# A decoder layer's distance bias, made on 128 partitions with 32x32 products and two VectorE additions, after norm1's output instead of before it

## The chip, the cores and the metric

The kernel is one program on one core of a Trainium2 chip. TensorE (PE, with its weight loads PEld), VectorE (DVE), ScalarE (ACT) and GpSimd (POOL) each run their own list of instructions in order. Transfers are issued in order by SyncE (SP) and by GpSimd, and run on 16 DMA engines. The metric is the device time of the whole program in microseconds.

## What is computed

A decoder layer for a prompt of 1024 tokens and 8 sequences of 8 new tokens (1088 tokens in all, float32). Cut to what matters here:

```
m = split(silu(c) @ w_ada + b_ada, 6)                  # shift, scale, gate: per sequence
h = rms_norm(x, norm1_g) * (1 + scale1) + shift1       # norm1's output
z = h @ w_in                                           # q | k | v | u, 2048 columns
logits = q . k + rel_bias[rel_bucket(distance)]        # three (window, dilation) branches
x = x + gate1 * (concat(attention, pool) @ w_out)
x = x + gate2 * (relu(h2 @ w_up) ** 2 @ w_down)
```

The bias of a head at a distance is one of 32 table entries. The kernel adds to it the logarithm of the number of branches that hold the distance, or -1e30 where none does. This is needed once for 2312 + 1440 distances and 8 heads.

## The kernel before

Everything is kept with the channels on partitions, in tiles of 128 x 1088. float32 products of the large layers are made as three products of rounded halves (high x high, low x high, high x low: lines L243, L245, L247), each in three pieces of 512, 288 and 288 columns.

**Stage 1** loads the eight tiles of x (`xT`), squares and adds them up on ScalarE and VectorE, and makes the reciprocal root `rstd1` (function `rstd_of`: a product with ones, `Ln` and `Exp` on ScalarE, three VectorE steps, each in two pieces). Beside it run the first products of `w_ada` (`ada_mm`, L101): eight loads `wa0_0_k` of 512 KB give `pa0_0`, which is copied (`adas`, L107), transposed (`pat`, L110) and added into `aT`. From `aT` and `rstd1` comes `h1h`/`h1l`, the high and low half of norm1's output: `h1_half(0)` makes tiles 0 to 3, `h1_half(1)` tiles 4 to 7 (VectorE makes `hp` and `h1l`, ScalarE `h1h`).

**Stage 2** multiplies with `w_in`. Its tile m is loaded (`win{m}r`, 512 KB), cast to the high half on ScalarE and subtracted to the low half; its outputs are `z{m}_0` to `z{m}_2`. Tiles 4 and 5 begin with h1 tiles 0 to 3, with the second `w_ada` products (`wa0_1_k`, `pa0_1`) between them. After `pa0_1` follows **the turn**: its copy, transposition, `aT`, `h1_half(1)`; then tiles 4 and 5 go on with h1 tiles 4 to 7, and the w_in tiles 6, 7, 0, ... follow. The remaining `w_ada` loads (`wa1_r_k`) go along, two for each w_in tile, and share four buffers of 512 KB (tag "raw") with the w_in loads: a load waits on SyncE's queue until the buffer's last reader is done, and everything behind it on the queue waits too.

**The bias** is made in stage 1. `rbias` (32 x 8) and four one-hot tiles `oh` (32 x 1024) are loaded, eight products (L224) of 8 rows by 512 columns write the banks `pg0` and `pg512`, ScalarE copies the pieces out to `fb` (L228), and GpSimd adds them to the logarithms `lm` (L302), 8 partitions at a time. After the last `h1l` (the copy to `mark`, L304, waits for it) GpSimd issues five transfers that write `lm` to the DRAM scratch `gscr` (each head 16 times) and `fscr` (L309, L312). Their result is read back much later.

TensorE's, VectorE's and ScalarE's orders here are set by a scheduler that weaves the program's statements; `tc.issue_after` holds some statements back. SyncE's order comes out of the same scheduler.

Of the kernel before, what the change touches and what calls it, by code (L numbers as in the profile page):

```python
# [11 lines left out]
F32 = mybir.dt.float32  # L12
# [5 lines left out]
P = 128  # L18
# [7 lines left out]
H = 8  # L26
# [12 lines left out]
GLEN = 2312  # L39
FLEN = 15 * 96  # L40
GREP = 16
# [4 lines left out]
CTX = 15  # L46
# [3 lines left out]
def body(ctx: ExitStack, tc: tile.TileContext, i, o):  # L50
    nc = tc.nc
    mm = nc.tensor.matmul
    V = nc.vector
    S = nc.scalar
    G = nc.gpsimd
# [4 lines left out]
    const = ctx.enter_context(tc.tile_pool(name="const", bufs=1))  # L60
    pools = {"": tc.alloc_tile_pool(name="psum1", bufs=8, space=PSUM)}
    wpool = ctx.enter_context(tc.tile_pool(name="wpool", bufs=3))

    def ps(name, tag="ps"):
        return pools[""].tile([P, 512], F32, tag=tag, name=name, bufs=PSB[tag])
# [5 lines left out]
    def part(name):  # L71
        c0, shape = CPK[name]
        n = math.prod(shape)
        v = cpk[:, c0:c0 + n]
        if len(shape) == 2:
            v = v.rearrange("p (a b) -> p a b", b=shape[1])
        return v

    cT, bT, g1T, g2T, qkg, ident, ones, sel, selb, pscT, rcnt = (part(n) for n in CPK)
    gq = const.tile([P, 1], F32, tag="gq", name="gq")  # L80
    V.tensor_scalar_mul(gq, qkg[:, 0:1], E ** -0.5)
    gk = qkg[:, 1:2]
# [10 lines left out]
    def ada_load(r, hf, k, pool, tag, bufs):  # L93
        t = pool.tile([P, 2, 512], F32, tag=tag, name=f"wa{r}_{hf}_{k}", bufs=bufs)
        src = i["w_ada"][k * P:(k + 1) * P, r * 2048:(r + 1) * 2048].rearrange("p (s c) -> p s c", s=2)
        nc.sync.dma_start(t, src[:, :, hf * 512:(hf + 1) * 512])
        return t

    def ada_mm(pa, k, t):
        for g in range(4):  # L100
            ins = mm(pa[32 * g:32 * g + 32, :256], cs[:, k, :], t[:, g // 2, (g % 2) * 256:(g % 2 + 1) * 256],  # L101
                     start=(k == 0), stop=(k == KD - 1))
        return ins

    def ada_end(r, hf, pa):
        sb = (wpool if r else nat_pool).tile([P, 256], F32, tag="tmp" if r else "nat", name=f"adas{r}_{hf}", bufs=2 if r else NNAT)
        act = S.copy(sb, pa[:, :256])  # L107
        pt = ps(f"pat{r}_{hf}")
        for j in range(2):
            nc.tensor.transpose(pt[:, j * P:(j + 1) * P], sb[:, j * P:(j + 1) * P], ident)  # L110
        for j in range(2):
            src = pt[:, j * P:(j + 1) * P].rearrange("p (s q c) -> p s q c", s=2, c=32)[:, :, :, 0:9]
            idx = aT[:, r * 16:(r + 1) * 16, :].rearrange("p (s h q j) c -> p s h q j c", s=2, h=2, q=2)
            bb = bT[:, r * 16:(r + 1) * 16].rearrange("p (s h q j) -> p s h q j", s=2, h=2, q=2)[:, :, hf, :, j]
            V.tensor_tensor(idx[:, :, hf, :, j, :], src, bb.unsqueeze(3).to_broadcast([P, 2, 2, 9]), ALU.add)
        return act
# [43 lines left out]
    nat_pool = tc.alloc_tile_pool(name="nat", bufs=NNAT, side="left")  # L160
# [11 lines left out]

    gscr = tc.dram_tile([H, GREP, GLEN], F32, name="gscr")
    fscr = tc.dram_tile([H, FLEN], F32, name="fscr")
    rbias = const.tile([32, H], F32, tag="rbias", name="rbias")
    nc.sync.dma_start(rbias, i["rel_bias"])
    lm = nat_pool.tile([P, 1024], F32, tag="nat", name="lm")
    G0 = [(32 * n, c0, min(1024, GLEN + FLEN - c0)) for n, c0 in enumerate(range(0, GLEN + FLEN, 1024))]
    ohs = []
    for r0, c0, n in G0:  # L180
        oh = wpool.tile([32, 1024], F32, tag="wf", name=f"oh{c0}", bufs=NWF)
        nc.sync.dma_start(oh[:, :n], i["onehot"][:, c0:c0 + n])
        nc.sync.dma_start(lm[r0:r0 + H, :n], i["logmult"][:, c0:c0 + n])
        ohs.append(oh)
    wa0 = {(0, k): ada_load(0, 0, k, *(((wpool, "raw", NRAW), (nat_pool, "nat", NNAT))[k // 4])) for k in range(KD)}

    xs = nat_pool.tile([P, KD, NB, TS], F32, tag="nat", name="xs")
# [1 line left out]
    for k in range(KD):  # L189
        if k == 0:  # L190
            S.activation(acc, xts[0], AF.Square)
        else:
            sq = wpool.tile([P, T], F32, tag="tmp", name=f"xsq{k}", bufs=2)
            act = S.activation(sq, xts[k], AF.Square)
# [3 lines left out]
    def rstd_of(acc, rstd, chunks, name):  # L198

        a0, a1 = chunks[0][0], chunks[-1][0] + chunks[-1][1]  # L200
        vv = wpool.tile([P, T], F32, tag="tmp", name=f"{name}v", bufs=2)
        tv = wpool.tile([P, T], F32, tag="tmp", name=f"{name}t", bufs=2)
        for ci, (c0, n) in enumerate(chunks):
            pp = ps(f"{name}_{ci}")
            ins = mm(pp[:, :n], ones, acc[:, c0:c0 + n], start=True, stop=True)
            V.tensor_scalar(vv[:, c0:c0 + n], pp[:, :n], 1.0 / D, EPS, ALU.mult, ALU.add)
        half = [slice(a0, a0 + 512), slice(a0 + 512, a1)] if a1 - a0 > 600 else [slice(a0, a1)]
        for c in half:
            ln = S.activation(tv[:, c], vv[:, c], AF.Ln)
        with tc.issue_after(ln.ins):  # L210
            for c in half:
                S.activation(rstd[:, c], tv[:, c], AF.Exp, scale=-0.5)
        for c in half:
            newton(rstd[:, c], vv[:, c], tv[:, c])
        return ins

    fb = wpool.tile([P, 1024], F32, tag="wf", name="fb", bufs=NWF)
    pgs = []
    for d0 in (0, 512):
        pg = ps(f"pg{d0}")  # L220
        for (r0, c0, n), oh in zip(G0, ohs):
            if n > d0:
                w = min(512, n - d0)
                pe = mm(pg[r0:r0 + H, :w], rbias, oh[:, d0:d0 + w], start=True, stop=True)  # L224
                pgs.append((pg, slice(r0, r0 + H), d0, w))
    with tc.issue_after(act.ins):
        for pg, r, d0, w in pgs:
            S.copy(fb[r, d0:d0 + w], pg[r, :w])  # L228
    pa = ps("pa0_0")
    with tc.issue_after(pe.ins):  # L230
        pe = ada_mm(pa, 0, wa0[0, 0])
    with tc.issue_after(pe.ins):
        pe = rstd_of(acc, rstd1, CHUNKS, "n1")
    with tc.issue_after(pe.ins):
        for k in range(1, KD):
            pe = ada_mm(pa, k, wa0[0, k])
# [52 lines left out]
    act = ada_end(0, 0, pa)  # L289
# [3 lines left out]
    pa = ps("pa0_1")  # L293
# [4 lines left out]
            ada_mm(pa, k, wa0[1, k])  # L298
    ada_end(0, 1, pa)
    h1_half(1)  # L300
    for r0, c0, n in G0:
        G.tensor_add(lm[r0:r0 + H, :n], lm[r0:r0 + H, :n], fb[r0:r0 + H, :n])  # L302
    mark = const.tile([P, 1], F32, tag="mark", name="mark")
    ins = G.tensor_copy(mark, f(h1l[KD - 1][:, 0:1]))  # L304
    with tc.issue_after(ins.ins):
        for r0, c0, n in G0:
            ng = max(0, min(n, GLEN - c0))
            if ng:
                G.dma_start(gscr[:, :, c0:c0 + ng], lm[r0:r0 + H, :ng].unsqueeze(1).to_broadcast([H, GREP, ng]))  # L309
            if ng < n:  # L310
                f0 = c0 + ng - GLEN
                G.dma_start(fscr[:, f0:f0 + n - ng], lm[r0:r0 + H, ng:n])  # L312

    later_ada = ada_steps()

# [67 lines left out]
    for hp in range(HP):  # L383
        r0 = 32 * hp
# [125 lines left out]
    for hp in range(HP):  # L510
        for a in range(2):
            r0 = a * E
# [447 lines left out]

CPK, NCPK = {}, 0
for _n, _s in (("cT", (KD, 9)), ("bT", (48,)), ("g1T", (KD,)), ("g2T", (KD,)), ("qkg", (2,)), ("ident", (P,)),
               ("ones", (P,)), ("sel", (32,)), ("selb", (P,)), ("pscT", (4,)), ("rcnt", (4, CTX))):
    CPK[_n] = (NCPK, _s)
    NCPK += math.prod(_s)

# [5 lines left out]
NWF = 6  # L972
# [6 lines left out]
def _distance_tables():  # L979


    far = WB + 7 - np.arange(15)[:, None] - 16 * np.arange(96)[None]
    dist = np.concatenate([GOFF - np.arange(GLEN), far.ravel()])
    d = np.maximum(dist, 1).astype(np.float32)
    large = 16 + (np.log(d / np.float32(16)) / np.float32(math.log(2048 / 16)) * np.float32(16)).astype(np.int32)
    bucket = np.where(dist < 16, dist, np.minimum(large, 31))
    onehot = ((bucket[None, :] == np.arange(32)[:, None]) & (dist >= 0)[None]).astype(np.float32)
    n = sum(((dist >= 0) & (dist <= w) & (dist % s == 0)).astype(np.int64) for w, s in ((128, 1), (512, 4), (2048, 16)))
    logm = np.where(n > 0, np.log(np.maximum(n, 1)), BIG).astype(np.float32)
    return onehot, np.ascontiguousarray(np.broadcast_to(logm, (H, GLEN + FLEN)))  # L990


def _tiles(w, m):
# [90 lines left out]
```

## Time and profile before

| | us |
|---|---|
| median of three runs | 1384.89 (1379.83 to 1388.64) |
| the profiled execution | 1382.63 |
| its span, first to last instruction | 1380.9 |
| TensorE busy | 1316.5 (95%) |
| VectorE, ScalarE, GpSimd busy | 583.8, 390.4, 118.8 |

The span is what the trace covers; 1.7 us of the execution's time lies around it. Times in rows count from the span's start. "Idle before, releaser" in a row is the time that the engine stood still before it, and what ended that.

### The profile page before, as it was taken

The page shows a single profiled execution, that of the slowest core. Times are in us where ns is not written, and L with a number is a line of the kernel's source. Part 1 is how long each engine was busy: PE and PEld are TensorE (multiplying, and loading weights), DVE is VectorE, ACT ScalarE, POOL GpSimd, SP SyncE. Part 2 cuts the span into 40 slices and gives each one's busy share as a digit, 9 for nine tenths or more (in the row PEclk, how much of TensorE's full clock was granted, in tenths as well). Part 3 has the DMA queues.
Part 4 walks back from the last instruction along what each step waited for, and adds up shares of the span by engine and source line. Part 5 has one row for each costly group of instructions (what it writes and reads, how often), then busy time and mean ns, then how long its engine had stood idle before and what let it go on. Part 6 is the DMA issues. An engine that isn't in the chain of part 4 may idle for free.

```text
span 1380.9 us, 21237 instructions
## 1 busy us (share of the span) xinstructions
PE 1316.5 (95%) x9060; PEld 1106.6 (80%) x9060; DVE 583.8 (42%) x1120; ACT 390.4 (28%) x660; POOL 118.8 (9%) x168
## 2 busy tenths in 40 slices
PE   3699999789999999999999999999999999999998
PEld 1486868575665558999999999999999999999998
DVE  4744152215656564567332433433433324334333
ACT  5233121115757553435202102112012012021120
POOL 3202006221112000000000000000000000000000
PEclk9899999897999999999999999999999999999999
DMA  9785352958667564482961631721813615411102
GB/s 289 236 123 178 104 168 36 142 165 316 225 222 267 161 218 141 131 280 79 328 202 47 202 133 47 266 68 47 277 44 135 198 47 190 145 47 47 31 33 98
DMA packets 56671, 210.96 MB, mean 153 GB/s; under 512 B 14576, under 2 KB 14832, under 8 KB 55552
## 3 DMA queue, kind: packets, MB, share of 16 engines
q1 hardware_dynamic: 52688, 136.72, 31.9%
q0 software_dynamic: 3888, 72.87, 16.7%
q8 instruction: 71, 1.16, 0.4%
q14 instruction: 24, 0.20, 0.0%
HBM read 199.15 MB, written 77.27 MB: 200 GB/s over the span
## 4 chain that ended last, share of the span: by engine, by line
PE 89%; DMA 5%; DVE 2%; ACT 2%; SPq 1%; issue 1%; DVEq 0%; ACTq 0%
PE dn L245 9%; PE dn L247 9%; PE dn L243 9%; PE up L243 9%; PE up L247 9%; PE up L245 9%; PE z L243 4%; PE z L247 4%; PE z L245 4%; PE pt L702 2%; PE po L712 2%; PE S L657 2%; DMA wa<-in_w_ada 1%; PE spo L615 1%; PE sl L569 1%; PE ob L243 1%
## 5 line engine op out<-in xcount | busy, mean ns | idle before, releaser
L827 DVE SCALAR_TENSOR_TENSOR X<-dn,aT,X 128x512 f32<-128x512 f32 (+2 forms) x192 | 98.4, 567 | 204.6 <-PE dn L247 204.6
L859 POOL COPY mark<-fh 128x1 f32<-128x1 f32 x7 | 8.5, 1218 | 562.3 <-ACT fh L926 562.3
L927 DVE TENSOR_TENSOR fl<-r,fh 128x1088 fp32r<-128x1088 f32 x32 | 41.3, 1292 | 35.5 <-ACT fh L926 35.5
L525 ACT ACTIVATE L<-L,m 128x128 f32<-128x128 f32 (+7 forms) x64 | 49.1, 769 | 21.7 <-DVE m L529 21.7
L705 ACT COPY PT<-pt 128x512 f32<-128x512 f32 (+1 forms) x80 | 41.7, 541 | 39.3 <-PE pt L702 30.5
L702 PE MATMUL pt<-cpk,L 128*128 128x128 f32 x288 | 45.4, 284 | 2.6 <-ACT PT L705 1.5
L926 ACT CAST fh<-r 128x1088 fp32r<-128x1088 f32 x32 | 35.4, 1105 | 44.1 <-DVE r L923 44.1
L702 PEld LDWEIGHTS pt<-cpk,L 128*128 128x128 f32 x288 | 31.1, 141 | 18.0 <-issue 11.1
L101 PE MATMUL pa<-wa,cs 128*32 128x256 f32 x384 | 30.8, 403 | 13.7 <-DMA wa<-in_w_ada 13.6
L245 PE MATMUL dn<-fh,wd_3l 128*128 128x288 f32 (+1 forms) x192 | 43.4, 328 | 0.0
L247 PE MATMUL dn<-fl,wd_3h 128*128 128x288 f32 (+1 forms) x192 | 43.4, 328 | 0.0
L243 PE MATMUL dn<-fh,wd_3h 128*128 128x288 f32 (+1 forms) x192 | 43.4, 328 | 0.0
L243 PE MATMUL dn<-fh,wd_1h 128*128 128x288 f32 (+1 forms) x192 | 42.5, 328 | 0.0
L245 PE MATMUL dn<-fh,wd_1l 128*128 128x288 f32 (+1 forms) x192 | 42.5, 328 | 0.0
L247 PE MATMUL dn<-fl,wd_1h 128*128 128x288 f32 (+1 forms) x192 | 42.3, 328 | 0.0
L245 PE MATMUL dn<-fh,wd_0l 128*128 128x288 f32 (+1 forms) x192 | 42.3, 328 | 0.0
L243 PE MATMUL dn<-fh,wd_0h 128*128 128x288 f32 (+1 forms) x192 | 42.2, 328 | 0.0
L247 PE MATMUL dn<-fl,wd_2h 128*128 128x288 f32 (+1 forms) x192 | 42.2, 328 | 0.0
L243 PE MATMUL dn<-fh,wd_2h 128*128 128x288 f32 (+1 forms) x192 | 42.2, 328 | 0.0
L245 PE MATMUL dn<-fh,wd_2l 128*128 128x288 f32 (+1 forms) x192 | 42.2, 328 | 0.0
L247 PE MATMUL dn<-fl,wd_0h 128*128 128x288 f32 (+1 forms) x192 | 42.1, 328 | 0.0
L529 DVE CUSTOM_DVE_ANT_0 L<-S,fs 128x384 f32<-128x384 f32 (+5 forms) x64 | 32.0, 537 | 23.9 <-PE S L657 23.8
(940 smaller groups left out, 3385.3 us busy)
## 6 DMA issues: line engine op xcount, KB each, us to landing
out_kw<-in_cache_k POOLq DMA_DIRECT2D x8, 4080.0 KB, 15.9
out_vw<-in_cache_v POOLq DMA_DIRECT2D x8, 4080.0 KB, 29.2
wa<-in_w_ada SPq DMA_DIRECT2D x48, 512.0 KB, 5.2
kc<-in_kc SPq DMA_DIRECT2D x40, 512.0 KB, 5.3
vc<-in_vc SPq DMA_DIRECT2D x40, 512.0 KB, 5.0
x<-in_xT SPq DMA_DIRECT2D x8, 544.0 KB, 9.0
X<-in_xT SPq DMA_DIRECT2D x8, 544.0 KB, 8.1
fs<-gscr SPq DMA_DIRECT2D x8, 512.0 KB, 8.2
```

The costliest lines, as they stand in the source:

```text
L101: ins = mm(pa[32 * g:32 * g + 32, :256], cs[:, k, :], t[:, g // 2, (g % 2) * 256:(g % 2 + 1) * 256], start=(k == 0), stop=(k == KD - 1))
L243: mm(pt[:, :n], wh[:, kw], xh(k, c0, n), start=st, stop=False)
L245: mm(pt[:, :n], wl[:, kw], xh(k, c0, n), start=False, stop=False)
L247: mm(pt[:, :n], wh[:, kw], xl(k, c0, n), start=False, stop=sp)
L525: last["act"] = S.activation(L[:, :n], L[:, :n], AF.Exp, bias=negm, scale=-1.0, accum_out=sm)
L529: V.tensor_tensor_reduce(out=L[:, c0:c0 + n], in0=pt, in1=bias, scale=-1.0, scalar=(3.0e38 if prev is None else prev), op0=ALU.add, op1=AL ...
L657: mm(pts[a][:, :nm], w[r, qc], m[r, c0:c0 + nm], start=(x == 0), stop=(x == 2))
L702: nc.tensor.transpose(pt[:, n * P:(n + 1) * P], u["L"][:, a, ii * nk0 + j * P:ii * nk0 + (j + 1) * P], ident)
L705: later(0, lambda: S.copy(PT[:, :n * P], pt[:, :n * P]))
L827: V.scalar_tensor_tensor(X[:, m, c0:c0 + npr], pt[:, :npr], aT[:, base + m, 0:1], X[:, m, c0:c0 + npr], ALU.mult, ALU.add)
L926: S.copy(fh, r)
L927: V.tensor_sub(fl, r, f(fh))
```

## The change

The bias is computed after `h1_half(1)` in the program's text. `rel_bias` comes with the constants `cpk` (32 more columns, the table once in each 32 partitions). The one-hot table and the logarithms come as one tile of 128 x 1024 each (512 KB each; rows 32n + head hold distances 1024n and on, the other rows are not used). Eight products of 32 x 32 by 512 columns write the two banks, and VectorE adds each bank to half of `lm`. ScalarE's copies and GpSimd's additions are gone. The five scratch writes are issued as before, from the same 8 of each 32 rows.

```diff
-    rbias = const.tile([32, H], F32, tag="rbias", name="rbias")
-    nc.sync.dma_start(rbias, i["rel_bias"])
-    lm = nat_pool.tile([P, 1024], F32, tag="nat", name="lm")
...
-    for r0, c0, n in G0:
-        oh = wpool.tile([32, 1024], F32, tag="wf", name=f"oh{c0}", bufs=NWF)
-        nc.sync.dma_start(oh[:, :n], i["onehot"][:, c0:c0 + n])
-        nc.sync.dma_start(lm[r0:r0 + H, :n], i["logmult"][:, c0:c0 + n])
...
-                pe = mm(pg[r0:r0 + H, :w], rbias, oh[:, d0:d0 + w], start=True, stop=True)
...
-    with tc.issue_after(act.ins):
-        for pg, r, d0, w in pgs:
-            S.copy(fb[r, d0:d0 + w], pg[r, :w])
     pa = ps("pa0_0")
-    with tc.issue_after(pe.ins):
-        pe = ada_mm(pa, 0, wa0[0, 0])
+    pe = ada_mm(pa, 0, wa0[0, 0])
...
     h1_half(1)
-    for r0, c0, n in G0:
-        G.tensor_add(lm[r0:r0 + H, :n], lm[r0:r0 + H, :n], fb[r0:r0 + H, :n])
+
+    oh, lm = [nat_pool.tile([P, 1024], F32, tag="nat", name=n) for n in ("oh", "lm")]
+    nc.sync.dma_start(oh, i["onehot"])
+    nc.sync.dma_start(lm, i["logmult"])
+    for d0 in (0, 512):
+        pg = ps(f"pg{d0}")
+        for r0 in range(0, P, 32):
+            mm(pg[r0:r0 + 32, :], rbias[r0:r0 + 32, :], oh[r0:r0 + 32, d0:d0 + 512], start=True, stop=True)
+        V.tensor_add(lm[:, d0:d0 + 512], lm[:, d0:d0 + 512], pg)
     mark = const.tile([P, 1], F32, tag="mark", name="mark")
```

The change moves instructions at three places. In the lists, x4 is four products, and a trailing number only tells tiles apart.

SyncE's queue behind the load of `wa1_0_2`, before:

```order
L96 DMA wa1_0_3_576<-in_w_ada 128x2x512
L152 DMA win6r_590<-in_w_in 128x1024
L96 DMA wa1_0_4_671<-in_w_ada 128x2x512
L96 DMA wa1_0_5_677<-in_w_ada 128x2x512
L152 DMA win7r_691<-in_w_in 128x1024
```

And after:

```order
L96 DMA wa1_0_3_554<-in_w_ada 128x2x512
L280 DMA oh_432<-in_onehot 128x1024
L281 DMA lm_433<-in_logmult 128x1024
L152 DMA win6r_568<-in_w_in 128x1024
L96 DMA wa1_0_4_649<-in_w_ada 128x2x512
L96 DMA wa1_0_5_655<-in_w_ada 128x2x512
L152 DMA win7r_669<-in_w_in 128x1024
```

The two new loads stand between `wa1_0_3` and `win6r`. `win6r` takes the buffer of `wa1_0_0` in both programs, `win7r` that of `wa1_0_3` before and of `wa1_0_2` after.

TensorE at the turn, before:

```order
L101 MATMUL pa0_1_326<-wa0_1_7_275,cs_68 32x256 x4
L110 MATMUL pat0_1_433<-cpk_64,adas0_1_431 128x128 x2
L101 MATMUL pa1_0_513<-wa1_0_0_514,cs_68 32x256 x4
L101 MATMUL pa1_0_513<-wa1_0_1_520,cs_68 32x256 x4
L101 MATMUL pa1_0_513<-wa1_0_2_570,cs_68 32x256 x4
L101 MATMUL pa1_0_513<-wa1_0_3_576,cs_68 32x256 x4
L243 MATMUL z4_0_288<-h1h4_249,win4h_284 128x512
```

And after:

```order
L101 MATMUL pa0_1_292<-wa0_1_7_241,cs_68 32x256 x4
L110 MATMUL pat0_1_399<-cpk_64,adas0_1_397 128x128 x2
L285 MATMUL pg0_436<-oh_432,cpk_64 32x512 x4
L285 MATMUL pg512_442<-oh_432,cpk_64 32x512 x4
L220 MATMUL z4_0_254<-h1h4_215,win4h_250 128x512
```

The bias products have taken the place of the four groups that read `wa1_0_0` to `wa1_0_3`.

Those groups on TensorE after, the last reader of `wa1_0_0`, 33 products behind `pg512`:

```order
L222 MATMUL z4_1_255<-h1h6_219,win4l_251 128x288
L222 MATMUL z4_2_256<-h1h6_219,win4l_251 128x288
L101 MATMUL pa1_0_491<-wa1_0_0_492,cs_68 32x256 x3
L101 MATMUL pa1_0_491<-wa1_0_1_498,cs_68 32x256
L224 MATMUL z4_0_254<-h1l6_220,win4h_250 128x512
```

and the readers of `wa1_0_2` and `wa1_0_3`, when the tiles 4 and 5 are done:

```order
L224 MATMUL z5_2_267<-h1l7_222,win5h_261 128x288
L101 MATMUL pa1_0_491<-wa1_0_2_548,cs_68 32x256 x4
L101 MATMUL pa1_0_491<-wa1_0_3_554,cs_68 32x256 x4
L220 MATMUL z6_0_574<-h1h0_207,win6h_570 128x512
```

So the buffers that `win6r` and `win7r` wait for are given back later than before. In the old order products of `z6` stood between those of `z4` and `z5`; now all of them stand behind, and the readers of `wa1_0_4` and `wa1_0_5` behind those.

## Rows read from the trace of the kernel before

**Rows 1.** The page's busy line, and the table by stretch: start:end, length, busy time (instructions) of PE, PEld, DVE, ACT, POOL, granted TensorE clock as a share, DMA busy share, GB/s.

```profile
PE 1316.5 (95%) x9060; PEld 1106.6 (80%) x9060; DVE 583.8 (42%) x1120; ACT 390.4 (28%) x660; POOL 118.8 (9%) x168
...
42.70:62.30 19.60, 19.36 (x136) 14.30 (x136) 10.93 (x13) 4.96 (x8) 3.43 (x1) 0.89 0.56 182
...
71.40:108.50 37.10, 37.10 (x221) 32.58 (x217) 13.26 (x22) 8.40 (x16) 5.83 (x11) 0.96 0.83 113
```

**Rows 2.** The chain of waits in the first 46 us: start, us, what.

```profile
18.34 4.48 PE pg L224 x14
26.96 0.30 ACT fb L228
27.27 1.20 ACT n1t L209 x2
30.45 3.52 DVE n1t L133 x2
33.97 2.69 DVE n1t L134 x2
38.18 2.02 DVE A L260
43.37 1.21 DVE h1l L279
```

**Rows 3.** VectorE and GpSimd in the same stretch: from the instructions by line and shape (count, busy, mean ns) and from the instructions in order of time.

```profile
L133 DVE SCALAR_TENSOR_TENSOR n1t<-rstd 128x576 f32<-128x576 f32 x1 | 2.9, 2895 | 0.0
L133 DVE SCALAR_TENSOR_TENSOR n1t<-rstd 128x512 f32<-128x512 f32 x1 | 0.7, 702 | 2.7 <-ACT rstd L212 2.7
19.85 1.29 DVE L195 TENSOR_TENSOR acc<-acc,xsq 128x1088 f32<-128x1088 f32 x1
25.77 0.69 DVE L206 TENSOR_SCALAR n1v<-n 128x512 f32<-128x512 f32 x1 [4.63 <-PE n L205]
25.81 9.64 POOL L302 TENSOR_TENSOR lm<-lm,fb 8x1024 f32<-8x1024 f32 x4 [7.37 <-ACT fb L228]
```

**Rows 4.** DMA in stage 1, by stretch of 2 us; columns as in rows 1.

```profile
16.00:18.00 2.00, 0.00 (x0) 0.00 (x0) 1.90 (x2) 1.72 (x2) 0.12 (x1) 1.00 0.55 97
18.00:20.00 2.00, 1.67 (x8) 0.62 (x12) 1.79 (x3) 1.21 (x2) 0.45 (x1) 1.00 0.33 84
...
22.00:24.00 2.00, 2.00 (x12) 0.55 (x10) 0.00 (x0) 1.18 (x3) 0.00 (x0) 1.00 1.05 405
```

**Rows 5.** The turn, instructions in order of time: start, us, engine, line, operation, tiles, [idle before, releaser].

```profile
63.82 1.28 DVE L264 SCALAR_TENSOR_TENSOR hp<-x,A,rstd 128x1024 f32<-128x1024 f32 x1
65.02 0.42 DVE L273 TENSOR_TENSOR xs<-xs,rstd 128x256 f32<-128x256 f32 x1
65.99 0.64 PE L101 MATMUL pa<-wa,cs 128*32 128x256 f32 x8 [1.34 <-DMA wa<-in_w_ada]
69.17 1.04 ACT L146 CAST win6h<-win6r 128x1024 fp32r<-128x1024 f32 x1 [2.88 <-DMA win6r<-in_w_in]
73.83 0.62 DVE L278 TENSOR_TENSOR h1l<-xs,h1h 128x64 fp32r<-128x64 f32 x4
75.57 2.58 DVE L279 SCALAR_TENSOR_TENSOR h1l<-hp,aT,h1h 128x1024 fp32r<-128x1024 f32 x2
```

**Rows 6.** SyncE's and GpSimd's transfers from the turn on, in order of time; the first is the load `wa1_0_3`, issued when the last product of `pa0_1` has read its buffer.

```profile
62.35 0.37 SPq L96 DMA_DIRECT2D wa<-in_w_ada  x1
66.69 0.34 SPq L152 DMA_DIRECT2D win7r<-in_w_in  x1
76.42 0.34 SPq L152 DMA_DIRECT2D win0r<-in_w_in  x1
78.34 2.03 POOL L309 DMA_DIRECT2D gscr<-lm  x3
87.42 10.04 SPq L96 DMA_DIRECT2D wa<-in_w_ada  x2
105.88 0.59 POOL L389 DMA_DIRECT2D bs<-gscr  x1 [24.45 <-DMA gscr<-lm]
```

**Rows 7.** DMA by stretch while `gscr` is written (columns as in rows 1), the time from issue to landing of the `wa` load issued in 80 to 112 us (the query on the tile), and two issue rows on another pair, by page and query: GpSimd's `out_vw` (issued at 579.7 us) and the load `wu1r` (issued at 587.73 us), KB each and us to landing.

```profile
88.00:92.00 4.00, 4.00 (x24) 2.99 (x23) 2.98 (x5) 2.39 (x5) 0.00 (x0) 1.00 0.92 45
102.00:104.00 2.00, 2.00 (x14) 1.82 (x14) 0.00 (x0) 0.00 (x0) 0.00 (x0) 1.00 1.03 271
...
DMA to landing us min/median/max: 19.9/19.9/19.9
...
out_vw<-in_cache_v POOLq DMA_DIRECT2D x8, 4080.0 KB, 29.2
wu1r<-in_w_up SPq DMA_DIRECT2D x1, 512.0 KB, 22.5
```

**Rows 8.** The prices of products: the products of `win7` (their count, ns, first and last start), a `w_ada` pair of groups in order of time, and the granted clock by 1 us around TensorE's restart at 42.7 us.

```profile
L243 PE MATMUL z<-h1h,win7h x24: 293/297/400, 96.6 to 107.4; 128*128 128x288 f32 x16, 128*128 128x512 f32 x8
L247 PE MATMUL z<-h1l,win7h x24: 293/297/400, 97.6 to 108.4; 128*128 128x288 f32 x16, 128*128 128x512 f32 x8
57.04 1.07 PE L101 MATMUL pa<-wa,cs 128*32 128x256 f32 x16
46.00:47.00 1.00, 1.00 (x5) 0.90 (x4) 1.00 (x1) 0.00 (x0) 1.00 (x1) 0.50 0.42 150
48.00:49.00 1.00, 1.00 (x18) 0.50 (x13) 1.00 (x2) 0.75 (x1) 0.00 (x0) 1.00 0.66 106
```

More of the change, by code (lines that the diff above doesn't have):

```diff
@@ L77, in part @@
         return v
-    cT, bT, g1T, g2T, qkg, ident, ones, sel, selb, pscT, rcnt = (part(n) for n in CPK)
+    cT, bT, g1T, g2T, qkg, ident, ones, sel, selb, pscT, rcnt, rbias = (part(n) for n in CPK)
     gq = const.tile([P, 1], F32, tag="gq", name="gq")
@@ L174, in body @@
     fscr = tc.dram_tile([H, FLEN], F32, name="fscr")
-    rbias = const.tile([32, H], F32, tag="rbias", name="rbias")
-    nc.sync.dma_start(rbias, i["rel_bias"])
-    lm = nat_pool.tile([P, 1024], F32, tag="nat", name="lm")
-    G0 = [(32 * n, c0, min(1024, GLEN + FLEN - c0)) for n, c0 in enumerate(range(0, GLEN + FLEN, 1024))]
-    ohs = []
-    for r0, c0, n in G0:
-        oh = wpool.tile([32, 1024], F32, tag="wf", name=f"oh{c0}", bufs=NWF)
-        nc.sync.dma_start(oh[:, :n], i["onehot"][:, c0:c0 + n])
-        nc.sync.dma_start(lm[r0:r0 + H, :n], i["logmult"][:, c0:c0 + n])
-        ohs.append(oh)
     wa0 = {(0, k): ada_load(0, 0, k, *(((wpool, "raw", NRAW), (nat_pool, "nat", NNAT))[k // 4])) for k in range(KD)}
@@ L215, in rstd_of @@
         return ins
[L217 to L223, printed above, removed]
-                pe = mm(pg[r0:r0 + H, :w], rbias, oh[:, d0:d0 + w], start=True, stop=True)
-                pgs.append((pg, slice(r0, r0 + H), d0, w))
-    with tc.issue_after(act.ins):
-        for pg, r, d0, w in pgs:
-            S.copy(fb[r, d0:d0 + w], pg[r, :w])
     pa = ps("pa0_0")
-    with tc.issue_after(pe.ins):
-        pe = ada_mm(pa, 0, wa0[0, 0])
+    pe = ada_mm(pa, 0, wa0[0, 0])
     with tc.issue_after(pe.ins):
@@ L305, in body @@
     with tc.issue_after(ins.ins):
-        for r0, c0, n in G0:
-            ng = max(0, min(n, GLEN - c0))
+        for n in range(4):
+            r, c0 = slice(32 * n, 32 * n + H), 1024 * n
+            w = min(1024, GLEN + FLEN - c0)
+            ng = max(0, min(w, GLEN - c0))
             if ng:
-                G.dma_start(gscr[:, :, c0:c0 + ng], lm[r0:r0 + H, :ng].unsqueeze(1).to_broadcast([H, GREP, ng]))
-            if ng < n:
+                G.dma_start(gscr[:, :, c0:c0 + ng], lm[r, :ng].unsqueeze(1).to_broadcast([H, GREP, ng]))
+            if ng < w:
                 f0 = c0 + ng - GLEN
-                G.dma_start(fscr[:, f0:f0 + n - ng], lm[r0:r0 + H, ng:n])
+                G.dma_start(fscr[:, f0:f0 + w - ng], lm[r, ng:w])
     later_ada = ada_steps()
@@ L962 @@
 for _n, _s in (("cT", (KD, 9)), ("bT", (48,)), ("g1T", (KD,)), ("g2T", (KD,)), ("qkg", (2,)), ("ident", (P,)),
-               ("ones", (P,)), ("sel", (32,)), ("selb", (P,)), ("pscT", (4,)), ("rcnt", (4, CTX))):
+               ("ones", (P,)), ("sel", (32,)), ("selb", (P,)), ("pscT", (4,)), ("rcnt", (4, CTX)), ("rbias", (32,))):
     CPK[_n] = (NCPK, _s)
@@ L989, in _distance_tables @@
     logm = np.where(n > 0, np.log(np.maximum(n, 1)), BIG).astype(np.float32)
-    return onehot, np.ascontiguousarray(np.broadcast_to(logm, (H, GLEN + FLEN)))
+    pad = ((0, 0), (0, 4096 - GLEN - FLEN))
+    onehot = np.pad(onehot, pad).reshape(32, 4, 1024).transpose(1, 0, 2).reshape(P, 1024)
+    return onehot, np.repeat(np.pad(logm[None], pad).reshape(4, 1024), 32, 0)
 def _tiles(w, m):
@@ L1030 @@
         "rcnt": np.broadcast_to(rc, (P, 4, CTX)),
+        "rbias": np.tile(np.pad(np.asarray(rel_bias), ((0, 0), (0, 32 - H))), (4, 1)),
     }
@@ L1035 @@
         "w_ada": np.asarray(w_ada)[0],
-        "rel_bias": np.asarray(rel_bias),
         "onehot": onehot,
```

## The prediction

> **What bounds the kernel now.** TensorE is busy for 1316.5 of 1380.9 us and almost without a gap after the first 72 us [rows 1], so the change is worth what it does to the moments at which TensorE stands still. I read three places: the table by stretch, which says where TensorE waits; the chain of waits in the first 46 us; and the transfers around the scratch writes of the bias.
>
> In the first stage the bias lies on the chain [rows 2]: its products take 4.48 us from 18.34, the last of ScalarE's copies ends at 27.26, and `Ln` starts 0.01 us later. From there `rstd1`, `A1` and norm1's output follow, and the dense products of tiles 4 and 5 only begin with the first `h1l` at 44.58. From 71.4 to 108.5 TensorE has no gap at all [rows 1], although DMA in 88 to 92 moves 45 GB/s at a busy share of 0.92 [rows 7]. Those are the scratch writes `gscr`, issued at 78.34; their reader on GpSimd waits until 105.88 [rows 6]. No load disturbs TensorE there because `win7r` was issued at 66.69 and `win0r` at 76.42, ahead of them [rows 6].
>
> **What goes away.** Nine small loads, ScalarE's eight copies and GpSimd's four additions leave the first stage; eight products move out of it. The sum of squares ends at 21.14 (19.85 + 1.29) [rows 3]. VectorE's first step behind the product with ones came at 25.77 [rows 3], 2.95 after the bias products ended, a `w_ada` group among that. The same 2.1 to 3.0 us behind 21.14 put that step at 23.2 to 24.1 and, with its 0.69, `Ln` at 23.9 to 24.8 where it was 27.27: 2.5 to 3.4 us sooner. Then VectorE: a step of 576 columns took 2895 ns beside GpSimd's additions, one of 512 took 702 beside none [rows 3]; 576 at that rate are 790, so 2.1 us more. The two steps behind it took 2.69 together [rows 2] and are taken at 1.3 without GpSimd (by bytes like the two of 702 and 790, so 1.2 to 1.5): up to 1.4 more, nothing if they stay as they are. The norm path gains 4.6 to 6.9 us. The weights' path gains too: from 16 to 20 us DMA moved 97 and 84 GB/s where it moves 405 with the `wa0` loads queued [rows 4]; filling that gap is worth (405 - 90)/405 x 4 = 3.1 us. That path had some slack in front of `aT`. The low half of `win4` stays on GpSimd and still holds VectorE for a few us (`A1` took 2.02 for 36 columns [rows 2]). I take 5.0 us for the turn, with ends of 3.1 and 6.9. TensorE is busy for 19.36 of 19.60 us between the first product and the turn [rows 1], so the gain arrives there whole.
>
> **What comes in, from the turn T on** (T is the issue of `wa1_0_3`, 62.35 in the old trace [rows 6]; times are T+).
>
> *The wait for the table.* `oh` stands on SyncE's queue behind `wa1_0_3`, which waits for the last product of `pa0_1`. `wa1_0_3` landed at 65.95, T+3.6 (TensorE's wait for it ends at 65.99 [rows 5]); the next 524 KB at 405 GB/s [rows 4] need 1.3 more: `oh` lands at T+5.0. TensorE's list is in order, so it stands still until then. Eight bias products took 4.48 us in the old trace [rows 2]; at a full clock, half of that. [...] In the old trace TensorE also reached its dense work only at 71.4, T+9.1 [rows 1]: the table's wait alone costs about nothing, up to 2 us if `oh` is late.
>
> *VectorE at the turn.* `hp` starts at T+1.5. Behind that stand four `hp` and four `h1l` of 1.28, three steps of 0.42, four small ones of 0.62 together [rows 5] and the two new additions. These have no row; the nearest is 0.69 for 512 columns out of a bank [rows 3], taken for each, with 0.45 (0.42 is the step of 256 columns) and 1.28 as ends. Sum 13.5; each start lies 0.08 before the last end (65.02 against 63.82 + 1.28), so the last `h1l` ends at about T+13.9 and `gscr` is issued at T+14.1. Before it was T+16.0 (78.34), because VectorE also waited behind `win6h` on ScalarE [rows 5].
>
> *The load `win6r`.* It waits for the last reader of `wa1_0_0`, which now stands 33 products behind the bias. Three products of one h1 tile (1088 columns) take 0.50 us: 72 products of `win7` run from 96.6 to 108.5 [rows 8]. The 33 hold 11,680 columns, 5.4 us, and the `wa` group is 0.5 (half of 1.07) [rows 8]: T+9.4 + 5.9 = T+15.3. So `win6r` is issued 1.2 us behind `gscr`; `wa1_0_4`, `wa1_0_5` and `win7r` later still.
>
> *What a load behind `gscr` costs.* The `wa` issued at 87.42 [rows 6] landed 19.9 us later, at 107.3 [rows 7]; while it waited, DMA moved 45 GB/s before and after its issue, and 271 only from 102 on. Loads behind GpSimd's window copies show the same: `wu1r` took 22.5 us, until the 29.2 us of `out_vw` were over [rows 7]. So `win6r` lands 107.3 - 78.34 = 29.0 us behind the issue of `gscr`: T+43.1; its cast is 1.04 [rows 5]; `z6` starts at T+44.2. TensorE has finished tiles 4 and 5 at T+9.4 + 11.9 + four groups of 0.5 + 0.5 of slow clock = T+23.8 and has nothing else in its list: it stands still for 20 us. Then `z6`, 11.9 and 2.3 for 4.7 us at half clock [rows 8], two `wa` groups 1.0, `z7` 11.9: T+71.3. Before, `z7` was done at 108.5, T+46.1. **That is 25.2 us lost, less 5.0 gained: 20.2 slower.** Behind `z7` the order is as before; TensorE's gaps to 260 us come from other transfers that shift along.
>
> The sum stands against the profiled execution: 1382.6 + 20.2 = 1402.8, of which 1.7 us lie around the span. The median of the runs is 2.3 us above that execution, inside their scatter; I say 1403.
>
> [...]
>
> **The rivals.**
>
> *A. As above, slower.* For it: the 19.9 us row, and the places of the waits in the order. Decided by `win6r` being behind `gscr`.
>
> *B. `win6r` slips through.* If the clock holds through the idle time, the bias products take 2.2 and `win6r` is issued at T+13.1, a us ahead of `gscr`; `win0r` was 1.9 ahead and came through [rows 6]. Then `z6` runs on time, but `win7r`, which waits for the end of tiles 4 and 5, is caught for certain: three loads behind the writes, the first landing at T+43.1, two more at 1.3 each, cast, `z7` with a slow start: T+43.1 + 2.6 + 1.0 + 11.9 + 2.3 = T+60.9, 14.8 lost, 9.8 slower: 1392. Against it: an idle time of four us in TensorE just ahead.
>
> *C. Loads and scratch writes share the engines.* If a load's pieces alternate with those of the writes, `win6r` and `win7r` land within TensorE's 11.9 us for a tile and nothing waits: tiles 4 and 5 end at T+23.8, `z7` at T+23.8 + 11.9 + 1.0 + 11.9 = T+48.6; 2.5 lost, 5.0 gained: 1380, the change's plain gain less the wait for the table. For it: the row of 19.9 us is of a load issued 9 us into the writes, not at their beginning. Against it: both rows of waiting loads [rows 7]. [...]
>
> **How the numbers follow.** A 0.64, B 0.17, C 0.14; 0.05 for something else. A's own terms (turn 3.1 to 6.9, landing up to 3 us earlier, slow clock 1 to 2.3) make it 1396 to 1408. From 1389 to 1409 the range holds A and most of B and leaves out C. One per cent, 13.8 us, is about what runs of this kernel can tell from no change. A is slower by more than that nearly always; B and C lie within it. Slower 0.62, same 0.35, faster 0.03.
>
> **What the profile would show.** Right: the first dense z products some 5 us sooner; TensorE waiting for `oh` some 4 us at the turn; ScalarE's `win6h` waiting for its load while DMA moves 45 GB/s, and a gap of about 20 us ahead of `z6`. In B the gap, about 10 us, stands ahead of `z7`. In C there is none. Wrong would be: `win6r` issued early, `gscr` later than the last `h1l` by my sum, or the scratch writes shorter than 23 us.

## The result and the profile after

The changed kernel takes 1405.15 us (median of 4 runs, 1401.03 to 1407.26); the kernel before took 1382.83 beside it. The ratio is 1.0138 with a 95% interval of 1.0113 to 1.0163. The profiled execution took 1404.2 with a span of 1402.5; before it was 1382.6 and 1380.9.

The page's busy line and the table by stretch answer to [rows 1] (columns as there). The stretches are: first products to the turn, the turn, tiles 4 and 5, the gap, tiles 6 and 7.

```profile
PE 1318.0 (94%) x9060; PEld 1111.4 (79%) x9060; DVE 580.2 (41%) x1122; ACT 386.2 (28%) x652; POOL 108.4 (8%) x164
...
37.50:57.10 19.60, 19.38 (x136) 13.88 (x135) 10.49 (x12) 4.91 (x8) 3.10 (x1) 0.89 0.55 182
57.10:65.75 8.65, 3.99 (x19) 0.94 (x19) 7.66 (x12) 3.41 (x8) 0.00 (x0) 0.80 0.51 185
65.75:81.30 15.55, 15.50 (x107) 11.80 (x104) 6.66 (x12) 3.45 (x5) 3.27 (x6) 1.00 0.53 30
81.30:98.30 17.00, 0.01 (x1) 0.01 (x1) 0.03 (x1) 1.04 (x1) 0.00 (x0) 0.64 0.83 105
98.30:125.90 27.60, 27.60 (x160) 24.11 (x160) 6.41 (x9) 4.51 (x8) 6.72 (x12) 0.91 0.49 148
```

TensorE's busy time is what it was. Between the end of tile 5 and the start of tile 6 it stands still for 17.0 us; [rows 1] has no gap there. The granted clock falls to 0.50 within the gap, and tile 6 begins at that level; from 104 us it is at 1.00 again.

Instructions in order of time (start, us, engine, line, operation, tiles, count, [idle before, releaser]), first one of before, then of the changed kernel:

```profile
33.90 2.77 DVE L134 TENSOR_TENSOR n1t<-n1t,n1v 128x512 f32<-128x512 f32 x2
...
28.06 1.36 DVE L133 SCALAR_TENSOR_TENSOR n1t<-rstd 128x512 f32<-128x512 f32 x2 [2.69 <-ACT rstd L202]
32.21 2.34 DVE L237 SCALAR_TENSOR_TENSOR A<-aT,cpk 128x36 f32<-128x36 f32 x1
...
57.12 0.37 ACT L107 COPY adas<-pa 128x256 f32<-128x256 f32 x1 [10.42 <-PE pa L101]
...
62.20 1.07 PE L285 MATMUL pg<-oh,cpk 32*32 32x512 f32 x4 [4.22 <-DMA oh<-in_onehot]
...
71.31 2.03 POOL L295 DMA_DIRECT2D gscr<-lm  x3
...
72.72 0.33 SPq L152 DMA_DIRECT2D win6r<-in_w_in  x1
...
97.20 1.04 ACT L146 CAST win6h<-win6r 128x1024 fp32r<-128x1024 f32 x1 [20.63 <-DMA win6r<-in_w_in]
...
98.30 1.27 PE L220 MATMUL z<-h1h,win6h 128*128 128x512 f32 x3 [17.05 <-ACT win6h L146]
```

The steps on VectorE that took 3.52 [rows 2] and 2.77 beside GpSimd's additions take 1.36 each without them, the turn comes at 57.12 instead of 62.35, and the bias products wait 4.22 for `oh`. Then `win6r` is issued 1.4 us behind the first `gscr` write, and TensorE waits for its cast.

The DMA queues (packets, MB, share of 16 engines) in 87 to 91 and 91 to 95 us, q0 GpSimd's, q1 SyncE's, and the landing of `win6r` in us:

```profile
q0 software_dynamic: 51, 0.21, 98.5%
...
q0 software_dynamic: 222, 0.19, 51.5%
q1 hardware_dynamic: 196, 0.51, 32.2%
...
DMA to landing us min/median/max: 24.5/24.5/24.5
```

From 75 to 91 us q1 moved no packet at all, although `win6r` had been issued at 72.72. From 91 on it moves.

### The profile page after: what moved, and what is told of

Read it like the earlier page. It is cut to its first block, busy times and chain, and to the rows that moved or that the text cites. A ratio compares the mean times of both kernels' runs of the same rounds, so it can differ in the third digit from the quotient of the medians.

```text
span 1402.5 us, 21216 instructions
## 1 busy us (share of the span) xinstructions
PE 1318.0 (94%) x9060; PEld 1111.4 (79%) x9060; DVE 580.2 (41%) x1122; ACT 386.2 (28%) x652; POOL 108.4 (8%) x164
## 4 chain that ended last, share of the span: by engine, by line
PE 88%; DMA 6%; DVE 3%; ACT 1%; SPq 1%; issue 1%; DVEq 0%; ACTq 0%
PE dn L222 9%; PE dn L224 9%; PE dn L220 9%; PE up L220 9%; PE up L222 9%; PE up L224 9%; PE z L220 5%; PE z L222 4%; PE z L224 4%; PE po L698 2%; PE pt L688 2%; PE S L643 2%; DMA win6r<-in_w_in 2%; PE spo L601 1%; DMA wa<-in_w_ada 1%; PE sl L555 1%
## 5 line engine op out<-in xcount | busy, mean ns | idle before, releaser
L912 ACT CAST fh<-r 128x1088 fp32r<-128x1088 f32 x32 | 35.3, 1103 | 44.2 <-DVE r L909 44.2
L688 PEld LDWEIGHTS pt<-cpk,L 128*128 128x128 f32 x288 | 31.1, 141 | 17.8 <-issue 10.9
L101 PEld LDWEIGHTS pa<-wa,cs 128*32 128x32 f32 x384 | 10.3, 111 | 42.6 <-ACT xsq L184 17.4
```

Of the source, the lines that this page charges most:

```text
L688: nc.tensor.transpose(pt[:, n * P:(n + 1) * P], u["L"][:, a, ii * nk0 + j * P:ii * nk0 + (j + 1) * P], ident)
L912: S.copy(fh, r)
```

## The experiments

T is the ScalarE copy at the turn, about 57 us in the kernels built on the changed one. "Landed" is counted from the issue of `win6r`.

| kernel | us, median | ratio to before (95%) | `win6r` to first `gscr` issue | landed | TensorE's wait before z6 |
|---|---|---|---|---|---|
| changed kernel | 1405.2 | 1.0138 (1.0113 to 1.0163) | 1.4 behind | 24.5 | 17.0 |
| writes behind tile 5 | 1387.1 | 1.003 (1.001 to 1.0049) | 9.0 ahead | 3.6 | 0 |
| writes from 32 partitions | 1382.1 | 0.9998 (0.9976 to 1.0019) | 1.6 behind | 8.0 | 0.6 |
| `gscr` written twice | 1415.6 | 1.0241 (1.0191 to 1.0291) | 1.7 behind | 23.1 | 15.7 |
| pieces of 1 KB | 1388.8 | 1.0037 (1.0016 to 1.0059) | 1.8 behind | 12.3 | 4.9 |
| tables loaded early | 1376.0 | 0.9961 (0.9943 to 0.998) | 9.0 ahead | 3.7 | 0 |
| both: early, 32 partitions | 1376.2 | 0.9954 (0.9939 to 0.997) | 9.0 ahead | 3.7 | 0 |
| writes on ScalarE's queue | 1394.2 | 1.0075 (1.0049 to 1.01) | 8.6 behind | 18.3 | 10.9 |

### Writes held back behind tile 5

```diff
-    ins = G.tensor_copy(mark, f(h1l[KD - 1][:, 0:1]))
+            ins = G.tensor_copy(mark, kT[1][:, T - 1:T])
```

The copy and the writes below it now stand behind `kg.tile(1)`.

> The scratch writes are taken out of their place behind the last h1l and issued behind the evacuation of tile 5 (mark copies a column of the finished k tile 1 instead of h1l); everything else is as in the changed kernel. T is the issue of wa1_0_3, 57.12 in the changed kernel's trace. Theory (a load issued behind the writes waits until they end): the writes are issued at about T+26, win6r (T+15.6) lands some 4 us after its issue, TensorE waits for no load between tiles 5 and 7, z7 ends at about T+49 where it ended at T+68.8, and the time is 1380 to 1386 us. win0r, issued at about T+36, is caught until T+52, under the statistics of k, which cover it. Rival (the table's wait, the order of TensorE's list or the clock cost the time): the 17.0 us before z6 shrink by less than half, and the time stays above 1395.

1387.1 us. GpSimd's writes, ScalarE's cast of `win6r`, and TensorE's one wait for a load, of 79 to 125 us:

```profile
81.94 2.02 POOL L351 DMA_DIRECT2D gscr<-lm  x3
...
76.55 1.05 ACT L146 CAST win6h<-win6r 128x1024 fp32r<-128x1024 f32 x1 [7.39 <-DMA win6r<-in_w_in]
...
111.24 1.08 PE L101 MATMUL pa<-wa,cs 128*32 128x256 f32 x8 [3.87 <-DMA wa<-in_w_ada]
```

Everything else of the change is in place, and the wait before z6 is gone: the order of TensorE's list and the table's wait did not make the 17 us. The time ends a little above the range expected. Loads behind the held writes are late instead: a `w_ada` load, for which TensorE waits 3.87, and `win0r` (issued at 94.25, cast at 112.9), to which no wait of TensorE is put down.

### Writes that read 32 partitions

```diff
-"rbias": np.tile(np.pad(np.asarray(rel_bias), ((0, 0), (0, 32 - H))), (4, 1)),
+"rbias": np.tile(np.asarray(rel_bias), (4, 4)),
...
-G.dma_start(gscr[:, :, c0:c0 + ng], lm[r, :ng].unsqueeze(1).to_broadcast([H, GREP, ng]))
+G.dma_start(gscr[:, :, c0:c0 + ng].rearrange("r p c -> p r c"),
+            lm[32 * n:32 * n + 32, :ng].unsqueeze(1).to_broadcast([32, 4, ng]))
```

The scratch tile is laid out anew with it (the heads inside the copies), and the addresses of its readers follow.

> The scratch tile keeps its contents but is laid out with the heads inside the copies, the table rbias holds the 8 heads four times over in its 32 columns instead of once and zeros, so that the 32x32 products make four copies of each head's bias row on 32 partitions at no cost, and each write reads 32 partitions, each four times, instead of 8 partitions 16 times. Bytes, number of transfers and their place are unchanged. If what makes the writes slow (45 GB/s) is reading few partitions, they run up to four times as fast, end about 8 us behind their issue instead of 26, win6r lands by T+24 and the 17.0 us before z6 fall below 3: 1382 to 1388 us. If the rate does not depend on the partitions read, all stays as it was, 1405.

1382.1 us, the time of the kernel before. TensorE's waits at the bias products and before z6, GpSimd's queue from 73 to 74 us, and the landing of `win6r`:

```profile
62.63 3.40 PE L285 MATMUL pg<-oh,cpk 32*32 32x512 f32 x16 [4.67 <-DMA oh<-in_onehot]
82.06 0.76 PE L220 MATMUL z<-h1h,win6h 128*128 128x512 f32 x3 [0.60 <-ACT win6h L146]
...
q0 software_dynamic: 48, 0.20, 93.5%
...
DMA to landing us min/median/max: 8.0/8.0/8.0
```

The same bytes move at 0.20 MB a us (200 GB/s) instead of 0.05: four times the partitions read, four times the rate. The order of the rows in DRAM changed along with the partitions, and no run here has one without the other. `win6r` still stands behind the writes, but lands after 8.0.

### The writes made twice, and in shorter pieces

```diff
+                for scr in (gscr, gscr2):
-                G.dma_start(gscr[:, :, c0:c0 + ng], ...)
+                    G.dma_start(scr[:, :, c0:c0 + ng], ...)
```

> Each gscr write is made twice, the second time into a scratch tile that nobody reads: twice the bytes on the same queue, the same place. Theory that a load waits until all writes end: the writes last some 50 us from 71.3, win6r lands near 121 instead of 97, the wait before z6 grows from 17 to some 41 us, the time to 1428 to 1432 us. If a load waits only for the writes issued ahead of it (two of five in the changed kernel), its wait grows by less than half of that: under 1418.

1415.6 us (two runs). The row of z6, then the queues in 86 to 90, 90 to 94 and 102 to 106 us:

```profile
95.95 1.28 PE L221 MATMUL z<-h1h,win6h 128*128 128x512 f32 x3 [15.73 <-ACT win6h L146]
...
q0 software_dynamic: 51, 0.21, 94.7%
...
q0 software_dynamic: 312, 0.17, 62.6%
q1 hardware_dynamic: 139, 0.52, 31.5%
...
q0 software_dynamic: 52, 0.21, 96.1%
q1 hardware_dynamic: 52, 0.11, 6.8%
```

My theory in its plain form falls here: `win6r` landed after 23.1 us, no later than with half the writes, in the middle of them. From 90 to 94 q1 passes 139 packets (0.52 MB, the size of `win6r`), and later, at 102 to 106, the two queues move 52 packets each. The other reading on record, a wait for only the writes issued ahead, had put the time under 1418. What is lost beyond the changed kernel is lost to the next loads (waits of 3.7, 5.4 and 1.4 before z7).

```diff
-                G.dma_start(gscr[:, :, c0:c0 + ng], ...)
+                for p0 in range(0, ng, 256):
+                    p1 = min(p0 + 256, ng)
+                    G.dma_start(gscr[:, :, c0 + p0:c0 + p1], ...)
```

> Each gscr write is cut along its columns into pieces of 256 numbers (1 KB instead of 4 KB each run), ten transfers in place of three. Theory that a load waits for the writes whatever their pieces: win6r lands near 97 again, the wait stays 15 to 20 us, 1402 to 1408 us. Rival (the engines take turns between the queues piece by piece, so that a load waits in proportion to the pieces' length): the landing of win6r falls from 24.5 to below 14 us, the wait to below 7, the time to below 1396.

1388.8 us. The queues in 78 to 79 and 81 to 82 us, and the landing of `win6r`:

```profile
q1 hardware_dynamic: 4, 0.02, 8.6%
...
q0 software_dynamic: 12, 0.05, 94.3%
q1 hardware_dynamic: 15, 0.06, 14.9%
...
DMA to landing us min/median/max: 12.3/12.3/12.3
```

The writes' rate is unchanged, yet the load's first packets come 5 us behind its issue and then alternate with the writes, 15 to 12 in that us. (12 packets of 0.05 MB: a packet of the trace holds 4 KB here too, four pieces.) So it isn't a fixed number of bytes ahead that holds the load; what shrank with the pieces is the length of each transfer. With 512 in place of 256:

> As e4_split, with pieces of 512 numbers (2 KB) in place of 256. If a load waits for a fixed number of pieces on each engine (16 of 4 KB at 1.28 us are the 20 us seen in the changed kernel, 16 of 1 KB the 5.2 us at which the first packets of win6r came in e4_split), its first packets come about 10 us behind its issue and it lands 15 to 19 us behind, the wait before z6 is 8 to 12 us, the time 1391 to 1397. If it waits for a fixed number of transfers or for all writes, it lands some 24 us behind its issue and the time is 1402 to 1408.

1397.1 us (ratio 1.0102, 1.0076 to 1.0128; runs from 1387.14 to 1399.91). The queues in 80 to 81 and 81 to 82 us, and TensorE's wait before z6:

```profile
q0 software_dynamic: 13, 0.05, 103.1%
...
q0 software_dynamic: 34, 0.03, 56.3%
q1 hardware_dynamic: 9, 0.04, 10.7%
...
PE z L220 <- ACT win6h L146: 5.4, 1, 5.4
```

The profiled execution is the fastest of these runs, so its wait of 5.4 is not that of the median; in it `win6r` landed after 12.8, sooner than the 15 to 19 expected. The first packets are what counts. The writes began between 71 and 74 us in all four kernels, and `win6r`'s first packets followed some 19 us later with pieces of 4 KB (91 to 92; 90 to 91 with twice the writes), 9 to 10 with 2 KB, 5 to 6 with 1 KB. A 4 KB piece takes 1.28 us on its engine (50 packets on 16 engines in 4 us), so sixteen of them take 20.5, and by their length sixteen of 2 and of 1 KB take 10.2 and 5.1: about sixteen pieces on each engine go first, then the load passes. Sixteen pieces are also two transfers, since each `gscr` transfer of these four kernels lays eight pieces on an engine (8 partitions 16 times, on 16 engines), whatever their length. So these kernels don't tell a hold by pieces from a hold by the first two transfers, and the 24 us that my expectation gave for a fixed number of transfers were worked out wrongly: shorter pieces make the transfers shorter too. Nor is the number fixed: in the kernel with wide writes `win6r` moved its first packets between 75 and 76 us, when 124 packets of 4 KB had been written, about eight on each engine.

### Tables loaded early

```diff
+    oh, lm = [nat_pool.tile([P, 1024], F32, tag="nat", name=n) for n in ("oh", "lm")]
+    nc.sync.dma_start(oh, i["onehot"])
+    nc.sync.dma_start(lm, i["logmult"])
     act = ada_end(0, 0, pa)
...
     h1_half(1)
-    oh, lm = [nat_pool.tile([P, 1024], F32, tag="nat", name=n) for n in ("oh", "lm")]
-    nc.sync.dma_start(oh, i["onehot"])
-    nc.sync.dma_start(lm, i["logmult"])
```

> The loads of oh and lm are written ahead of the copy adas0_0, so that SyncE issues them among the wa0_1 loads, long before the turn; the products, the additions and the scratch writes stay in the text where they are in the changed kernel, the writes still read 8 partitions at 45 GB/s. T is again the issue of the copy at the turn, about 57. TensorE then has the bias products ready at T and does not stand still for 4.2 us ahead of them; they run at the full clock (about 2.2 us), the dense products start some 4 us sooner, and win6r, which waits for the last product of wa1_0_0, is issued ahead of the scratch writes (these still wait for the last h1l, T+14). Theory (only loads issued behind the writes wait): win6r and probably win7r come through, TensorE waits for no load between tiles 5 and 7, z7 ends by T+47, 1373 to 1380 us; if win7r falls behind the writes, 8 to 10 us more, 1383 to 1390. Rival (the engines are shared, whatever the order of issue): the load still takes above 15 us and the time stays above 1390.

1376.0 us. The bias products, SyncE's two loads, GpSimd's writes, and the stretch 80 to 84 us:

```profile
56.96 1.92 PE L285 MATMUL pg<-oh,cpk 32*32 32x512 f32 x16
...
62.51 0.34 SPq L152 DMA_DIRECT2D win6r<-in_w_in  x1
67.98 0.34 SPq L152 DMA_DIRECT2D win7r<-in_w_in  x1
...
71.48 2.03 POOL L295 DMA_DIRECT2D gscr<-lm  x3
...
80.00:84.00 4.00, 4.00 (x32) 4.00 (x31) 0.00 (x0) 0.00 (x0) 0.00 (x0) 1.00 1.00 51
```

The writes are as slow as ever in 80 to 84, TensorE is busy throughout, because both loads went ahead of them by 9.0 and 3.5 us. The products take 1.92 at a granted clock of 1.00, and the kernel is faster than before.

> The early loads of e5_early together with the writes of e2_wide, which read 32 partitions. Against e2_wide the 4.7 us for which TensorE waited for oh go, and the slow clock behind them (about 1.7 us of the 3.4 that the products took): 1374 to 1378 us, faster than the kernel before by 0.3 to 0.6 per cent. If the writes no longer matter once the loads are ahead of them, this one and e5_early give the same time. If the table's wait was covered by other work, the time stays at 1382.

1376.2 us. The bias products take 1.92 here too. With the loads ahead, fast writes add nothing that can be measured. Against the kernel with wide writes alone (1382.1), early tables give 5.9 us: the price of the table's wait, with the slower products behind it (3.40 against 1.92) and the 0.60 before z6.

### The same wait made in the old kernel

```diff
-    ins = G.tensor_copy(mark, f(h1l[KD - 1][:, 0:1]))
+    ins = G.tensor_copy(mark, f(h1l[3][:, 0:1]))
```

> The kernel before, with one change: mark copies a column of the fourth h1l instead of the last, so that the scratch writes are issued some 24 us sooner, at about 54 instead of 78.3; their data are ready by then. Theory (a load issued behind the writes waits for up to 20 us): wa1_0_3, issued at 62.35 and landed at 65.95 before, and win6r behind it now land at 74 to 76, TensorE waits 8 to 10 us for them around the turn, and the old kernel becomes slower by as much, 1389 to 1394 us. Rival (the slowdown belongs to the products on 128 partitions or their place in TensorE's list): no change, 1380 to 1385.

1397.6 us (ratio 1.011, 1.0075 to 1.0145). GpSimd's writes, TensorE's wait and ScalarE's cast of `win6r`:

```profile
53.10 2.02 POOL L309 DMA_DIRECT2D gscr<-lm  x3
...
82.02 1.08 PE L101 MATMUL pa<-wa,cs 128*32 128x256 f32 x8 [18.68 <-DMA wa<-in_w_ada]
...
84.92 1.04 ACT L146 CAST win6h<-win6r 128x1024 fp32r<-128x1024 f32 x1 [19.51 <-DMA win6r<-in_w_in]
```

Issued 25 us sooner, the writes hold up the loads of the turn, and the old kernel loses 15.6 us: the mechanism needs nothing of the change. It is more than the 8 to 10 us that I expected: two `w_ada` loads (issued at 57 and 61 us) were caught ahead of `win6r`, and not only the last.

### The writes on ScalarE's queue, and behind tile 4

```diff
-                G.dma_start(gscr[...], ...)
+                S.dma_start(gscr[...], ...)
```

The two `fscr` writes move to that queue as well.

> The changed kernel with the five scratch writes issued by ScalarE's queue instead of GpSimd's; they still read 8 partitions in runs of 4 KB, and are issued behind the second lm addition, 1 to 3 us sooner than before. If the hold belongs to the engines (16 pieces that one queue has handed over go first, whichever queue it is), win6r's first packets come some 20 us behind the start of the writes and the wait before z6 stays 13 to 18 us: 1398 to 1406 us. If it belongs to GpSimd's queue alone, win6r alternates with the writes from the start, eight pieces an engine at 1.3 to 1.5 us each: it lands 11 to 14 us behind its issue, the wait falls to 3 to 7 us: 1386 to 1394 us.

1394.2 us, at the edge of the second range, but by neither of the two ways. The queues in 76 to 78 and 78 to 80 us (q10 is ScalarE's), and z6:

```profile
q10 hardware_dynamic: 25, 0.10, 48.3%
q1 hardware_dynamic: 64, 0.23, 36.9%
...
q10 hardware_dynamic: 27, 0.10, 46.4%
...
94.06 1.40 PE L220 MATMUL z<-h1h,win6h 128*128 128x512 f32 x3 [10.87 <-ACT win6h L146]
```

Here the writes use half of the engines (0.48 of 16) at the same 0.05 MB a us, twice as fast on each. The part of `win6r` on the free engines passes at once (64 packets of SyncE's queue in 76 to 78), the rest only from 90 us, when the two long writes end. So the hold is no property of GpSimd's queue; but on this queue it lasted for more than sixteen pieces: a transfer of 512 KB lays sixteen on each of its eight engines, and the two of them went first. The count of sixteen is not a rule. Two transfers fit this kernel and the four on GpSimd's queue compared above, but not the one with wide writes, where one went first; what sets the number stays open.

> As e1_hold, with the writes issued behind the evacuation of tile 4 instead of tile 5 (mark copies a column of k tile 0), some 5 us behind the last h1l, so that win6r (T+15.6) is issued 3 us ahead of them and win7r (T+24) 5 us behind. This is the rival case of the prediction in which win6r slips through. The writes begin at about T+19.5 and hold win7r until T+40 to T+42: z6 on time at T+24, then a wait of 4 to 6 us before z7; z7 ends at T+53 to T+56 instead of T+68.8: 1386 to 1392 us. If the order of issue did not matter, win6r would wait here as in the changed kernel and the time would stay above 1398.

1393.3 us (ratio 1.0069, 1.0046 to 1.0092; `mark` as in the first experiment, from k tile 0). SyncE's loads, GpSimd's writes, and the wait before z7:

```profile
73.80 0.33 SPq L152 DMA_DIRECT2D win6r<-in_w_in  x1
81.95 6.94 SPq L152 DMA_DIRECT2D win7r<-in_w_in  x1
...
77.46 2.02 POOL L351 DMA_DIRECT2D gscr<-lm  x3
...
105.08 1.08 PE L101 MATMUL pa<-wa,cs 128*32 128x256 f32 x8 [10.00 <-DMA wa<-in_w_ada]
```

The load ahead passes (landed after 3.5 us), those behind wait, as in my rival B. TensorE waits 10.0 and 1.4 before z7 where I expected 4 to 6 in all, and the time lies above the 1386 to 1392 expected.

## Why the prediction was right, and where its steps were off

It said 1403, in 1389 to 1409, by rival A; 1405 came, by that way. Its steps, in us behind T:

| step | predicted | measured |
|---|---|---|
| turn sooner by | 5.0 | 5.2 |
| `oh` ready, bias products start | 5.0 | 5.1 |
| bias products done | 9.4 | 8.6 |
| last `h1l` done, `gscr` issued | 13.9, 14.1 | 13.9, 14.2 |
| `win6r` issued | 15.3 | 15.6 |
| tiles 4 and 5 done | 23.8 | 24.1 |
| z6 starts | 44.2 | 41.2 |
| z7 done | 71.3 | 68.8 |

**The bias products** are in the sum at 4.4 us, from T+5.0 to T+9.4, for the slow clock of [rows 8] all through. No run shows that term for them: behind the wait for `oh` they took 3.55 us (62.20 to 65.75) at a mean granted clock of 0.52. Rival B's 2.2, half of the old 4.48, was an estimate too, since the trace before gives a clock of 1.00 at those products [rows 4]; at 1.00 the kernel with early tables took 1.92.

**The first stage** came out as worked: the first two of three steps on VectorE lost 2.2 and 1.4 (3.52 and 2.77 to 1.36 each), `A` starts at 32.21 instead of 38.18 [rows 2], 6.0 sooner where I had 4.6 to 6.9, and `A` itself still takes 2.34 beside GpSimd. Of the 6.0 the turn kept 5.2.

**The landing of `win6r`** was the term off most: 29.0 behind the issue of `gscr` by the row of the `wa` load [rows 7], measured 25.9. In that row SyncE's queue moved its first packets 24 us behind the issue of `gscr` (from 102 us), here 20 (from 91); what made the difference is not shown. The reason I gave ("until the writes end") was too broad: in this kernel the two `gscr` writes that go first (eight pieces of 4 KB an engine each) are nearly all that there is to write, so that waiting for them and waiting for the end came to the same; twice the writes told the two apart.

**The table's wait** I priced at "about nothing", because the old kernel too reached its dense work only at T+9.1. It costs 5.9 (above): in those 9 us the old kernel did products that the changed one does later. The sum had them at their later place, so its total was right while the sentence was wrong. Rival C, 1380, is the price of the change without the hold; the kernel with wide writes came to 1382.

**Behind z7** I expected no difference. z7 ends 17.4 us later than before (125.9 against 108.5), where the sum had 20.2; the span is 21.6 longer: 4.2 are lost later. That 1403 came so close to 1405 is in part luck: the landing too late by 3.1 and the loss behind z7 that the sum left out nearly cancel. TensorE by stretches of 3 us after z0, first of the changed kernel, then before:

```profile
147.00:150.00 3.00, 1.71 (x16) 0.81 (x12) 2.26 (x3) 1.04 (x1) 0.00 (x0) 1.00 0.95 281
150.00:153.00 3.00, 2.90 (x20) 1.11 (x20) 3.00 (x7) 0.00 (x0) 0.00 (x0) 0.67 0.99 370
153.00:156.00 3.00, 3.00 (x11) 1.87 (x8) 1.57 (x3) 1.04 (x1) 0.58 (x1) 0.50 0.99 364
```

```profile
132.00:135.00 3.00, 2.58 (x21) 1.05 (x22) 3.00 (x6) 0.00 (x0) 0.00 (x0) 1.00 0.97 343
```

Behind a wait of 1.4 for `w_ada` in the changed kernel the clock fell to 0.50; before, behind a wait of 0.8 at that place, it stayed at 1.00. But from the start of z7's last product to the end the profiled executions here took 1267.9 to 1281.7, among them 1273.4 with wide writes. That the 4.2 follow from the change is not shown.

**Turns between the queues.** Rival C had the pieces of loads and writes alternate. The runs show that too, but behind a stretch in which only the writes move: 15 packets to 12 in 81 to 82 us with pieces of 1 KB, 52 to 52 in 102 to 106 with twice the writes. In the changed kernel the load moves no packet from 75 to 91 us, which is against turns of one piece from the start. About sixteen pieces on each engine went ahead on GpSimd's queue, about eight with wide writes, more than sixteen on ScalarE's queue; what sets the number is not shown.

## What to carry to other kernels

A slow write was dear here not by its own length but by the loads issued just behind it: `win6r`, issued 1.4 us behind, landed after 24.5 us, issued 9.0 ahead after 3.7. Look up, for each write in the middle of a tight stretch, which loads stand within 20 us behind it (`win6r` moved no packet for 18 us here) and how long the tensor engine can go without them. Issue the loads ahead of it, or make it short: with 32 partitions read in place of 8, and the rows in another order, the writes ran at 0.20 MB a us instead of 0.05. And when a computation is moved, move its loads too: here the same change with its tables loaded early is 0.4% faster than the old kernel instead of 1.4% slower.

## What was unexpected of the hardware

The `gscr` writes that read 8 partitions ran at some 50 GB/s whether 16 engines carried them (1.28 us a piece of 4 KB) or 8 (0.62, on ScalarE's queue); from 32 partitions, with the rows in another order, they ran at 200. So the number of engines did not set the rate here; whether the partitions read or the order of the rows did is not shown.
